# One shared branch for the slots beyond 64: gate/up and down products of a column group leave it together

## The chip, the cores and the metric

One core of one Trainium2 chip runs the whole program in one launch. The time is device microseconds of that core; the kernel before was timed three times (1551.54, 1560.07 and 1565.84 us, median 1560.07).

## The reference, cut to what matters

The program is two transformer blocks over 256 tokens of width 1024, all in float32. The first block has a mixer, a dense feed-forward layer, a second mixer and a layer of 8 experts; each token goes to 2 of the 8:

```
for e in range(8):
    out = out + gate[:, e] * (silu(h @ wg[e]) * (h @ wu[e])) @ wd[e]      # 1024 -> 2816 -> 1024
```

The second block has attention, a short convolution and a layer of 16 small experts in 4 groups; each token goes to one group and to 2 of its 4 experts:

```
hid = silu(h @ w_gate[e]) * (h @ w_up[e]) * combine[:, e]                 # 1024 -> 256
out = out + hid @ w_down[e]                                               # 256 -> 1024
```

How many tokens an expert (or a group) gets is known only when the router has run on the chip.

## The kernel before, in words

**Slots.** The tokens of an expert (first layer), or of a group (second layer), are gathered into up to 96 slots: the first 64, and 32 more. An integer flag per expert says whether more than 64 slots are in use; only the tensor engine reads it (`more_than_half`, L887). In this text an expert with more than 64 tokens is a *full* expert, the others are *half* experts. In the trace the products of the slots beyond 64 (the matmuls of shape 128\*32) run for experts 2, 4, 5 and 6 of the first layer and for the third of the four groups of the second layer.

**Order of the work.** The 2816 hidden columns of an expert are cut into six column groups, in the order 0, 5, 1, 2, 3, 4 (positions 0 to 5); group 5 has 256 columns, the others 512. A *gu unit* (`bin_unit`, L962) multiplies the gathered tokens with the gate and up columns of a group; a *dn unit* (`bin_down`, L1010) multiplies the hidden values of a group with its rows of the down matrix and adds to two PSUM banks per expert. `ffn_order` (L69) puts the dn unit of a column group behind the gu unit of the next: gu 0, dn of the expert before, gu 5, dn 0, gu 1, dn 5, and so on. In the second layer an expert is one gu unit of 256 columns (two loads) and one dn unit (one load), in the same interleaving.

**A gu unit** runs its main matmuls (slots 0 to 63; two column halves side by side, so 128\*64) into bank `a`, then a branch: where the flag is set, four 128\*32 matmuls per row for the slots beyond 64 into bank `b` (L978); else one matmul with zeros into `b` (L984). Then `bin_mul` (L988) makes silu(gate) x up in three parts, each an activation on ScalarE (L996) and a multiplication on VectorE (L997): part 0 from bank `a`, parts 1 and 2 from bank `b`. Parts 1 and 2 run for every expert, full or half.

**A dn unit** runs its main matmuls, then a branch of its own (L1018): the products of the slots beyond 64, and else nothing, or a matmul with zeros where it is the first dn unit of the expert. Behind the dn unit `turn_hid` calls `bin_hid` (L1000): the tensor engine transposes the hidden values just made, first those of part 0 (L1004), then those of parts 1 and 2 (L1006), ScalarE copies them (L1007), and the dn unit after the next gu unit reads them. The order of each engine's instructions is the program's; an instruction that waits holds up all behind it on its engine.

**The stream.** Weights come in 1 MB loads through SyncE's queue, in the order of use, into 11 buffers that serve both expert layers. A buffer is loaded again when the matmuls that read it are done (`Stream.retire`, L225, says so in the program's order). Rows of most other layers are split into a high and a low part, by ScalarE (L197) and VectorE (L198), some rows ahead of their use: `W.ahead` rows, `AHEAD` = 4, and `AH1` = 2 from the last column group of expert 7 on. Rows of the experts are used as loaded.

**The end of a layer** is `last_down` (L1077): the last dn unit, `bin_y` (L1028: the sums are copied out of PSUM, L1031 to L1033), then for each half of the tokens `scatter` (L1036: products with one-hot matrices, and the addition to `x`, L1053 or L1051) and the transposes of `x` for the next layer.

Of the kernel before, what the change touches and what calls it, by code (L numbers as in the profile page):

```python
# [18 lines left out]
P = 128  # L19
T = 256  # L20
D = 1024
KT = D // P
# [5 lines left out]
RAW = 5  # L28
ROWS = 6
AHEAD = 4  # L30
AH1 = 2
RATE = 8
PE_TAPS = 11
OVER1 = 2
HALF = 64
MORE = 32
# [27 lines left out]
LAST = GROUPS[-1]  # L64
# [180 lines left out]
def block_kernel(ctx: ExitStack, tc: tile.TileContext, stream, x_in, cst_in, cols_in, small_in, sgu_in,  # L245
# [42 lines left out]
    W = Stream(nc, wp, stream, stream_order(), gcol)  # L288
# [52 lines left out]
    def mm(o, a, b, start, stop):  # L341
        nc.tensor.matmul(o, a, b, start=start, stop=stop)  # L342
# [544 lines left out]
    def more_than_half(got, e):  # L887

        if ("reg", e) not in got:
            got["reg", e] = nc.values_load(  # L890
                got["more"][0:1, e:e + 1], engines=[mybir.EngineType.PE], min_val=0, max_val=1,
                skip_runtime_bounds_check_because="the flag is the result of a comparison")
        return got["reg", e]
# [58 lines left out]
    def to_slots(pm, i, src, n):  # L952
# [6 lines left out]
        nc.vector.tensor_copy(t.rearrange("p j n -> p (j n)"), b[:, 0:3 * n])  # L959
        return t  # L960

    def bin_unit(xT, more, n, hooks=()):  # L962


        a, b = ps("gu"), ps("gu")
        kc, m = 512 // n, n // 2
        todo = []
        for r in range(KT // kc):
            row = W.take()
            for j in range(kc):  # L970
                k, at = kc * r + j, 2 * n * j
                todo.append((k, row, at))
                for h in range(2):
                    mm(a[h * HALF:(h + 1) * HALF, 0:n], xT[:, k, 0:HALF], row[:, at + h * n:at + (h + 1) * n], k == 0,
                       k == KT - 1)
            if r < len(hooks) and hooks[r]:
                hooks[r]()
        with tc.If(more == 1) as c:  # L978
            for k, row, at in todo:
                for q in range(4):  # L980
                    c0 = at + (q % 2) * n + (q // 2) * m
                    mm(b[q * MORE:(q + 1) * MORE, 0:m], xT[:, k, HALF:CAP], row[:, c0:c0 + m], k == 0, k == KT - 1)
        with c.Else():
            mm(b[:, 0:m], zeros[:, 0:P], zeros[:, 0:m], True, True)  # L984
        W.retire(KT // kc)
        return a, b

    def bin_mul(banks, n, s, h, gate, up):  # L988


        m = n // 2
        for (b, c0, m, lo, w, to, g, u) in ((banks[0], 0, n, 0, HALF, HALF, gate[0], up[0]),
                                            (banks[1], n, m, 0, MORE, MORE, gate[1], up[1]),
                                            (banks[1], n + m, m, HALF, MORE, MORE, gate[1], up[1])):
            t, v = s[lo + w:lo + 2 * w, c0:c0 + m], h[to:to + w, c0:c0 + m]
            nc.scalar.activation(t, b[lo:lo + w, 0:m], AF.Silu, scale=g[lo:lo + w])  # L996
            nc.vector.scalar_tensor_tensor(v, b[lo + w:lo + 2 * w, 0:m], u[lo + w:lo + 2 * w], t, op0=ALU.mult,  # L997
                                           op1=ALU.mult)
# [11 lines left out]
    def bin_down(hT, nk, more, dn, first, last):  # L1010


        rws = [W.take() for _ in range(nk)]
        for k in range(nk):
            for h in range(2):
                mm(dn[0][h * HALF:(h + 1) * HALF], hT[:, k, 0:HALF], rws[k][:, h * 512:(h + 1) * 512], first and k == 0,
                   last and k == nk - 1)
        with tc.If(more == 1) as c:  # L1018
            for k in range(nk):
                for q in range(4):  # L1020
                    mm(dn[1][q * MORE:(q + 1) * MORE, 0:T], hT[:, k, HALF:CAP], rws[k][:, q * T:(q + 1) * T],
                       first and k == 0, last and k == nk - 1)
        if first:
            with c.Else():
                mm(dn[1][:, 0:T], zeros[:, 0:P], zeros, True, True)
        W.retire(nk)

    def bin_y(dn):  # L1028

# [46 lines left out]

    def last_down(hT, nk, more, dn, pt, i, gate, nxt, fill=None):  # L1077

        bin_down(hT, nk, more, dn, False, True)
        y = bin_y(dn)  # L1080

        def spread(tb):
            scatter(pt, i, y, tb, more, gate(tb) if gate else None, "ms" if fill else "gu")

        if fill:
            fill(0)
        spread(0)
        W.pump(2)
        if fill:
            fill(1)  # L1090
        nxt.half(0, 0)
        spread(1)
        if fill:
            fill(2)
        nxt.half(0, 1)
        W.ahead = AHEAD
        W.pump()

    def moe1(cur, nxt):
# [44 lines left out]
        def moe1_tiles():  # L1144
            return sl("k5", [D]), sl("k6", [D])

        hid, fresh, dn, ydone = {}, [], None, None
        for kind, e, g, _ in ffn_order(BASE_MOE, NE):
            if e == NE - 1 and g == LAST:
                W.ahead = AH1  # L1150
            p, i = divmod(e, 2)
            pos = GROUPS.index(g)
            n = 512 if g < 5 else 256
            if kind == "gu" and e == 0 and g in DENSE:
                kw = cur.lead(_03=lambda: (route(0), cur.parts(0)), _10=lambda: route(1), _11=lambda: cur.parts(1),
                              _13=place)
                kw["hooks"] = [None] * 4 + [lambda: gather_pair(0, [0]), lambda: gather_pair(0, [1, 2]),
                                            lambda: gather_pair(0, [3])]
                banks = (pair_unit if g < 5 else half_unit)(cur.T, **kw)
                fresh.append((e, g, n, act_mul(banks, n, ("t2", "t3"), [rs(cur.gi, tb) for tb in range(2)])))  # L1160
            elif kind == "gu":
                hooks = [None] * 8
                if i == 1 and p < 3 and pos == 1:
                    pmq[p + 1] = one_hots(got["posm"], p + 1)
                if fresh:
                    hooks[0:3] = [lambda: slots_T(0), turn_hid, weights]
                if i == 1 and p < 3 and pos >= 2:
                    hooks[3] = lambda p=p, q=pos - 2: gather_pair(p + 1, [q])
                if i == 1 and p < 3 and g == LAST:
                    hooks[6] = lambda p=p: slots_T(p + 1)  # L1170
                if ydone is not None and pos == 2:
                    for tb in range(2):
                        hooks[1 + 4 * tb] = lambda tb=tb, a=ydone: scatter_e(*a, tb)
                    ydone = None
                banks = bin_unit(XT[p][:, :, i], more_than_half(got, e), n, hooks=hooks)
                s, h = moe1_tiles()
                r = RS[e]
                bin_mul(banks, n, s, h, (r[:, 0], r[:, 1]), (r[:, 0], r[:, 2]))
                fresh.append((e, g, n, h))
            elif e == NE - 1 and g == LAST:  # L1180
                last_down(hid[e, g], 4, more_than_half(got, e), dn, PT[p], i, lambda tb: gates[:, tb, e:e + 1], nxt)
            else:
                nk = 4 if g < 5 else 2
                if pos == 0:
                    dn = [ps("dn"), ps("dn")]
                bin_down(hid[e, g], nk, more_than_half(got, e), dn, pos == 0, g == LAST)
                if g == LAST:
                    ydone = (e, bin_y(dn))
            if fresh and kind == "dn":
                turn_hid()  # L1190
            if kind == "dn" and e == OVER1 and g == LAST:
                over = past(got["posm"], gates, NE, "p1")
                overflow(got["flag"], cur, over, NE, N_FFN, BASE_MOE,
                         [(5, 4, 4, 0, 22), (1, 2, 2, 20, 32)],
                         "xa" if e % 4 == 0 else "xb")
                nxt.load()
# [226 lines left out]
    def moe2(cur, nxt, fill):  # L1423
# [99 lines left out]
            else:  # L1523
                hid[e] = bin_hid(hs, T, t)

        hid, fresh, dn, ydone = {}, [], None, None

        def scatter_g(g, y, tb):
            scatter(PT[g // 2], g % 2, y, tb, more_than_half(got, g))
# [1 line left out]
        for kind, e in expert_order(16):  # L1531
# [13 lines left out]
            elif kind == "gu":  # L1545
# [11 lines left out]
                if ydone is not None and e % 4 == 2:  # L1557
                    for tb in range(2):
                        hooks[2 * tb] = lambda tb=tb, a=ydone: scatter_g(*a, tb)
                    ydone = None  # L1560
                banks = bin_unit(XT[p][:, :, i], more_than_half(got, g), T, hooks=hooks)
                s, h = sl(f"t{e % 2}", [512]), sl(f"t{2 + e % 2}", [512])
                c, j = CS[g], e % 4
                bin_mul(banks, T, s, h, (c[:, 0, 4:5], c[:, 1, 4:5]), (c[:, 0, j:j + 1], c[:, 2, j:j + 1]))
                fresh.append((e, h))
            elif e == 15:
                last_down(hid[e], 2, more_than_half(got, g), dn, PT[p], i, None, nxt, fill)
            else:
                if e % 4 == 0:
                    dn = [ps("dn"), ps("dn")]  # L1570
                bin_down(hid[e], 2, more_than_half(got, g), dn, e % 4 == 0, e % 4 == 3)
                if e % 4 == 3:
                    ydone = (g, bin_y(dn))
            if fresh and kind == "dn":
# [183 lines left out]
```

## Time and profile before

| what | us |
|---|---|
| runs | 1551.54, 1565.84, 1560.07 |
| median | 1560.07 |
| the profiled execution | 1551.7 |
| its span, first to last instruction | 1549.9 |
| tensor engine busy | 1488.1 (96%) |
| VectorE busy | 629.0 (41%) |
| ScalarE busy | 523.5 (34%) |
| mean DMA share of the span (hardware queue 1) | 71.0% |

The span is cut in two by the expert layers: the first layer's sorted experts run from about 436 us to 1140 us, the second's from about 1376 us to 1510 us. An engine that is busy is not necessarily at its peak: matmuls overlap and their ends are modelled, so lost time shows as a larger distance between the starts of matmuls. Times on the left of a timeline row are counted from the span's start.

### The profile page before, as it was taken

What the parts mean: (1) busy time and instruction counts of PE and PEld (TensorE: products, weight loads), DVE (VectorE), ACT (ScalarE), POOL (GpSimd) and SP (SyncE); (2) the same over time, 40 slices, a digit from 0 to 9 for tenths busy, and PEclk for the clock granted to TensorE, in tenths of its full rate; (3) what the DMA queues carried; (4) which work ended last, traced back from release to release, by engine and by line L of the source; (5) the groups of instructions that cost most, each with busy time, mean ns of one, the idle gap of its engine ahead of it and who ended that gap; (6) DMA issues with size and microseconds to landing.
All of it is one profiled execution on the core that took longest, in us unless ns stands there. A gap on an engine that the chain in (4) does not pass through costs nothing. (4 is left out here: it accounts for less than half of the span.)

```text
span 1549.9 us, 22973 instructions
## 1 busy us (share of the span) xinstructions
PE 1488.1 (96%) x9434; PEld 903.9 (58%) x9434; DVE 629.0 (41%) x1136; ACT 523.5 (34%) x856; POOL 127.1 (8%) x106
## 2 busy tenths in 40 slices
PE   7899999999999999989999999999989999999998
PEld 5778888877843334434444444444347888865546
DVE  6986655698511211112111111111247566732235
ACT  7645544584421111111111111111136555622134
POOL 4804000052100000000000000000002000100000
PEclk9999999999999999999999999999999999999999
DMA  8424555533479999998999987899984345478870
GB/s 320 163 109 170 192 196 203 183 137 136 179 302 414 414 412 415 396 387 348 412 390 363 391 309 290 327 360 379 416 334 143 133 163 193 140 303 324 324 276 28
DMA packets 84088, 429.05 MB, mean 277 GB/s; under 512 B 9328, under 2 KB 9840, under 8 KB 53488
## 3 DMA queue, kind: packets, MB, share of 16 engines
q1 hardware_dynamic: 83232, 425.01, 71.0%
q8 instruction: 102, 1.67, 0.4%
q10 hardware_dynamic: 720, 2.10, 0.3%
q14 instruction: 34, 0.28, 0.0%
HBM read 426.02 MB, written 1.05 MB: 276 GB/s over the span
## 5 line engine op out<-in xcount | busy, mean ns | idle before, releaser
L997 DVE SCALAR_TENSOR_TENSOR k<-gu,slots,k 64x512 f32<-64x512 f32 (+1 forms) x141 | 76.7, 544 | 404.1 <-ACT k L996 403.4
L996 ACT ACTIVATE k<-gu,slots 64x512 f32<-64x512 f32 (+1 forms) x141 | 72.4, 513 | 356.0 <-PE gu L342 324.7
L342 PE MATMUL gu<-whi,xah 128*128 128x512 f32 x528 | 180.3, 404 | 6.1 <-ACT whi L197 4.0
L198 DVE SCALAR_TENSOR_TENSOR wlo<-raw,cols,whi 128x1024 fp32r<-128x1024 f32 (+1 forms) x146 | 160.8, 1140 | 49.6 <-ACT whi L197 49.5
L342 PE MATMUL gu<-wlo,xah 128*128 128x512 f32 x528 | 174.2, 394 | 1.4 <-POOL wlo L203 1.1
L342 PE MATMUL gu<-whi,xal 128*128 128x512 f32 x528 | 173.7, 393 | 0.9 <-DVE xal L457 0.9
L197 ACT ACTIVATE whi<-raw,cols 128x1024 fp32r<-128x1024 f32 (+1 forms) x146 | 142.6, 1027 | 27.7 <-PE gu L342 18.3
L342 PE MATMUL dn<-raw,k 128*64 128x512 f32 (+1 forms) x856 | 127.8, 498 | 1.9 <-DMA raw<-in_stream_dram 1.2
L446 POOL TENSOR_TENSOR rcol<-rnv,mhalf 128x1 f32<-128x1 f32 x16 | 8.9, 555 | 1309.4 <-DVE rnv L445 1309.4
L342 PEld LDWEIGHTS gu<-whi,xah 128*128 128x128 f32 x528 | 97.5, 190 | 28.4 <-ACT whi L197 4.7
L342 PEld LDWEIGHTS gu<-wlo,xah 128*128 128x128 f32 x528 | 99.9, 189 | 23.6 <-POOL wlo L203 1.6
L342 PEld LDWEIGHTS gu<-whi,xal 128*128 128x128 f32 x528 | 99.8, 189 | 22.9 <-DVE xal L457 1.5
L342 PE MATMUL gu<-raw,xah 128*64 128x256 f32 (+3 forms) x944 | 103.3, 409 | 5.5 <-PEq L859 5.1
L342 PE MATMUL gu<-raw,xbh 128*64 128x256 f32 (+3 forms) x800 | 100.9, 439 | 2.7 <-DMA raw<-in_stream_dram 2.2
L202 ACT ACTIVATE whi<-raw 128x1024 fp32r<-128x1024 f32 x70 | 72.5, 1056 | 36.3 <-PE gu L342 31.8
L342 PEld LDWEIGHTS dn<-raw,k 128*64 128x64 f32 (+1 forms) x856 | 41.6, 124 | 72.9 <-issue 59.9
L342 PE MATMUL gu<-whiraw,xah 128*32 128x256 f32 (+3 forms) x552 | 82.8, 453 | 0.5 <-PEq L1042 0.4
L342 PE MATMUL gu<-wloraw,xah 128*32 128x256 f32 (+3 forms) x552 | 81.4, 447 | 0.0
L1007 ACT ACTIVATE k<-ms 128x384 f32<-128x384 f32 (+1 forms) x61 | 26.4, 433 | 146.4 <-PE ms L1006 145.9
L342 PEld LDWEIGHTS gu<-raw,xah 128*64 128x64 f32 (+1 forms) x944 | 46.2, 124 | 50.3 <-issue 32.3
L342 PE MATMUL gu<-whiraw,xbh 128*32 128x256 f32 (+2 forms) x448 | 73.5, 482 | 1.7 <-PEq L859 0.9
L342 PE MATMUL gu<-wloraw,xbh 128*32 128x256 f32 (+2 forms) x448 | 73.3, 480 | 1.2 <-DMA wloraw<-in_stream_dram 1.1
(318 smaller groups left out, 1988.8 us busy)
## 6 DMA issues: line engine op xcount, KB each, us to landing
raw<-in_stream_dram SPq DMA_DIRECT2D x238, 1024.0 KB, 8.6
whiraw<-in_stream_dram SPq DMA_DIRECT2D x164, 512.0 KB, 9.9
wloraw<-in_stream_dram SPq DMA_DIRECT2D x164, 512.0 KB, 10.1
x<-in_x_dram SPq DMA_DIRECT2D x2, 512.0 KB, 6.0
k<-in_lnrow_dram ACTq DMA_DIRECT2D x2, 512.0 KB, 7.5
cst<-in_cst_dram SPq DMA_DIRECT2D x1, 593.0 KB, 14.9
k<-in_gains_dram ACTq DMA_DIRECT2D x1, 512.0 KB, 7.7
out_dram<-k SPq DMA_DIRECT2D x2, 256.0 KB, 2.0
```

Of the source, the lines that this page charges most:

```text
L197: nc.scalar.activation(hi[:, c], raw[:, c], AF.Copy, scale=g)
L198: nc.vector.scalar_tensor_tensor(lo[:, c], raw[:, c], g, hi[:, c], op0=ALU.mult, op1=ALU.subtract)
L202: nc.scalar.activation(hi, raw, AF.Copy)
L342: nc.tensor.matmul(o, a, b, start=start, stop=stop)
L446: nc.gpsimd.tensor_tensor(rs(gi, tb), v, mhalf[:, :1], op=ALU.pow)
L996: nc.scalar.activation(t, b[lo:lo + w, 0:m], AF.Silu, scale=g[lo:lo + w])
L997: nc.vector.scalar_tensor_tensor(v, b[lo + w:lo + 2 * w, 0:m], u[lo + w:lo + 2 * w], t, op0=ALU.mult, op1=ALU.mult)
L1007: nc.scalar.activation(hT[:, 0:n // P], b[:, 0:n // P], AF.Copy)
```

## The change: what it does

Where a gu unit is followed by a dn unit of the same expert (positions 1 to 5 of the first layer; every expert but the first of its group in the second), the gu unit's branch is taken out of it and put behind the main matmuls of that dn unit, into one branch with the dn unit's products beyond 64. Its else arm holds the gu unit's matmul with zeros, and the dn unit's where there is one. Part 0 of `bin_mul` stays behind the gu unit's main matmuls; parts 1 and 2 come behind the shared branch, ahead of `turn_hid`. The buffers of the gu unit's rows are given back behind the shared branch. `AH1` becomes 0, so that no row of the next layer is split ahead of `bin_y` of expert 7, and the `W.pump(2)` of `last_down` becomes a `W.pump(1)` behind the first transposes.

```diff
-AH1 = 2
+AH1 = 0
+    def the_others(*parts):
+        with tc.If(parts[0][0] == 1) as c:
+            for _, others, _, _ in parts:
+                others()
+        if any(p[2] for p in parts):
+            with c.Else():
+                for _, _, none, _ in parts:
+                    if none:
+                        none()
+        W.retire(sum(p[3] for p in parts))
     def bin_unit(xT, more, n, hooks=()):
...
-        with tc.If(more == 1) as c:
+        def others():
             for k, row, at in todo:
                 for q in range(4):
...
-        with c.Else():
+        def none():
             mm(b[:, 0:m], zeros[:, 0:P], zeros[:, 0:m], True, True)
-        W.retire(KT // kc)
-        return a, b
+        return (a, b), (more, others, none, KT // kc)
-    def bin_mul(banks, n, s, h, gate, up):
+    def bin_mul(part, banks, n, s, h, gate, up):
...
     def bin_down(hT, nk, more, dn, first, last):
...
-        W.retire(nk)
+        return more, others, none if first else None, nk
     def last_down(hT, nk, more, dn, pt, i, gate, nxt, fill=None):
-        bin_down(hT, nk, more, dn, False, True)
+        the_others(bin_down(hT, nk, more, dn, False, True))
         y = bin_y(dn)
...
         spread(0)
-        W.pump(2)
...
         nxt.half(0, 0)
+        W.pump(1)
         spread(1)
# gu units of the first layer (the second's likewise, with e % 4 == 0)
-                bin_mul(banks, n, s, h, (r[:, 0], r[:, 1]), (r[:, 0], r[:, 2]))
+                mul(slice(0, 1))
+                if pos == 0:
+                    the_others(later)
+                    mul(slice(1, 3))
+                else:
+                    held = later, mul
# dn units
-                bin_down(hid[e, g], nk, more_than_half(got, e), dn, pos == 0, g == LAST)
+                parts = [bin_down(hid[e, g], nk, more_than_half(got, e), dn, pos == 0, g == LAST)]
+                if held:
+                    parts.insert(0, held[0])
+                the_others(*parts)
+                if held:
+                    held[1](slice(1, 3))
+                held = None
```

## Rows read from the trace of the kernel before

**Rows 1.** Windows: engines' busy us (instructions), granted clock, DMA share, GB/s, four stretches.
```profile
489.50:578.50 89.00, 82.14 (x409) 31.26 (x407) 16.52 (x33) 16.26 (x33) 0.00 (x0) 0.98 1.02 413
672.70:762.90 90.20, 83.80 (x457) 36.18 (x455) 16.70 (x34) 16.37 (x33) 0.00 (x0) 0.96 0.95 374
762.90:1062.40 299.50, 298.73 (x2746) 129.62 (x2744) 43.17 (x79) 42.28 (x85) 0.00 (x0) 0.99 0.91 352
1383.80:1438.20 54.40, 51.37 (x331) 30.57 (x328) 13.99 (x35) 14.77 (x35) 0.00 (x0) 0.94 0.81 299
```

**Rows 2.** Timeline of TensorE (start, us, what, idle before): a dn unit, full expert.
```profile
834.10 1.08 PE L342 MATMUL dn<-whiraw,k 128*64 128x512 f32 x4
...
836.73 1.03 PE L342 MATMUL dn<-wloraw,k 128*64 128x512 f32 x4
837.69 0.64 PE L342 MATMUL dn<-whiraw,k 128*32 128x256 f32 x8
...
839.55 0.46 PE L1004 MATMUL ms<-ident,k 64*128 64x64 f32 x4
...
840.30 1.08 PE L342 MATMUL gu<-whiraw,xbh 128*64 128x512 f32 x4
```

**Rows 3.** The same view: gu and dn unit of a half expert, 512 columns.
```profile
1102.34 3.60 PE L342 MATMUL gu<-raw,xah 128*64 128x512 f32 x16
1105.87 0.39 PE L342 MATMUL gu<-zeros 128*128 128x256 f32 x1
1106.18 3.65 PE L342 MATMUL dn<-raw,k 128*64 128x512 f32 x16
1110.00 0.43 PE L1004 MATMUL ms<-ident,k 64*128 64x64 f32 x4 [0.16 <-PEq L1018]
...
1110.72 1.51 PE L342 MATMUL gu<-raw,xah 128*64 128x512 f32 x6
```

**Rows 4.** Timeline of all engines: end of a gu unit's 128\*32 matmuls, parts 1 and 2.
```profile
849.72 1.26 PE L342 MATMUL gu<-raw,xbh 128*32 128x256 f32 x20
...
851.04 0.47 ACT L996 ACTIVATE k<-gu,slots 32x256 f32<-32x256 f32 x1 [2.93 <-PE gu L342]
...
852.05 0.47 ACT L996 ACTIVATE k<-gu,slots 32x256 f32<-32x256 f32 x1 [0.55 <-DVE k L997]
...
852.55 0.49 DVE L997 SCALAR_TENSOR_TENSOR k<-gu,slots,k 32x256 f32<-32x256 f32 x1 [0.53 <-ACT k L996]
```

**Rows 5.** Groups by form: parts 1 and 2 in units of 256 columns (busy, mean ns).
```profile
L996 ACT ACTIVATE t<-gu,slots 32x128 f32<-32x128 f32 x28 | 10.0, 358 | 12.9 <-DVE t L997 7.1 <-PE gu L342 5.5
...
L997 DVE SCALAR_TENSOR_TENSOR t<-gu,slots,t 32x128 f32<-32x128 f32 x28 | 9.8, 350 | 11.3 <-ACT t L996 11.0
```

**Rows 6.** Timeline of TensorE: units of the second layer, half group.
```profile
1499.67 0.30 PE L1004 MATMUL ms<-ident,t 64*128 64x64 f32 x2 [0.16 <-DVE t L997]
...
1500.14 1.08 PE L342 MATMUL gu<-whiraw,xah 128*64 128x256 f32 x8
...
1503.74 0.33 PE L342 MATMUL gu<-zeros 128*128 128x128 f32 x1
1504.00 1.08 PE L342 MATMUL dn<-whiraw,k 128*64 128x512 f32 x4
...
1506.10 0.31 PE L1004 MATMUL ms<-ident,t 64*128 64x64 f32 x2 [0.16 <-DVE t L997]
```

**Rows 7.** Timeline of TensorE: expert 3's second gu unit, behind the overflow branch.
```profile
691.42 5.09 PE L342 MATMUL gu<-raw,xah 128*64 128x256 f32 x32 [5.09 <-PEq L859]
```

**Rows 8.** Timelines of ScalarE and TensorE: the end of the first expert layer.
```profile
1140.22 2.19 ACT L197 ACTIVATE whi<-raw,cols 128x1024 fp32r<-128x1024 f32 x2 [4.16 <-DMA raw<-in_stream_dram]
1142.31 0.57 ACT L1031 ACTIVATE k<-dn 64x512 f32<-64x512 f32 x1
...
1142.94 1.12 PE L342 MATMUL gu<-k,sguT 64*128 64x512 f32 x2 [3.18 <-ACT k L1031]
```

**Rows 9.** Instructions of L1018: duration ns min/median/max, first and last start us.
```profile
L1018 PEldq COMPARE_BRANCH  x92: 63/179/2589, 438.5 to 1508.1; - x92
```

More of the change, by code (lines that the diff above doesn't have):

```diff
@@ L993, in bin_mul @@
                                             (banks[1], n, m, 0, MORE, MORE, gate[1], up[1]),
-                                            (banks[1], n + m, m, HALF, MORE, MORE, gate[1], up[1])):
+                                            (banks[1], n + m, m, HALF, MORE, MORE, gate[1], up[1]))[part]:
             t, v = s[lo + w:lo + 2 * w, c0:c0 + m], h[to:to + w, c0:c0 + m]
@@ L1017, in bin_down, with others @@
                    last and k == nk - 1)
-        with tc.If(more == 1) as c:
+        def others():
             for k in range(nk):
@@ L1022, in bin_down, with none @@
                        first and k == 0, last and k == nk - 1)
-        if first:
-            with c.Else():
-                mm(dn[1][:, 0:T], zeros[:, 0:P], zeros, True, True)
-        W.retire(nk)
+        def none():
+            mm(dn[1][:, 0:T], zeros[:, 0:P], zeros, True, True)
+        return more, others, none if first else None, nk
     def bin_y(dn):
@@ L1145, in moe1_tiles @@
             return sl("k5", [D]), sl("k6", [D])
-        hid, fresh, dn, ydone = {}, [], None, None
+        hid, fresh, dn, ydone, held = {}, [], None, None, None
         for kind, e, g, _ in ffn_order(BASE_MOE, NE):
@@ L1174, in moe1, with mul @@
                     ydone = None
-                banks = bin_unit(XT[p][:, :, i], more_than_half(got, e), n, hooks=hooks)
+                banks, later = bin_unit(XT[p][:, :, i], more_than_half(got, e), n, hooks=hooks)
                 s, h = moe1_tiles()
                 r = RS[e]
-                bin_mul(banks, n, s, h, (r[:, 0], r[:, 1]), (r[:, 0], r[:, 2]))
+                def mul(part, a=(banks, n, s, h, (r[:, 0], r[:, 1]), (r[:, 0], r[:, 2]))):
+                    bin_mul(part, *a)
+                mul(slice(0, 1))
[4 more added lines that the diff above has]
+                    held = later, mul
                 fresh.append((e, g, n, h))
@@ L1524, in turn_hid @@
                 hid[e] = bin_hid(hs, T, t)
-        hid, fresh, dn, ydone = {}, [], None, None
+        hid, fresh, dn, ydone, held = {}, [], None, None, None
         def scatter_g(g, y, tb):
@@ L1560, in moe2, with mul @@
                     ydone = None
-                banks = bin_unit(XT[p][:, :, i], more_than_half(got, g), T, hooks=hooks)
+                banks, later = bin_unit(XT[p][:, :, i], more_than_half(got, g), T, hooks=hooks)
                 s, h = sl(f"t{e % 2}", [512]), sl(f"t{2 + e % 2}", [512])
                 c, j = CS[g], e % 4
-                bin_mul(banks, T, s, h, (c[:, 0, 4:5], c[:, 1, 4:5]), (c[:, 0, j:j + 1], c[:, 2, j:j + 1]))
+                def mul(part, a=(banks, T, s, h, (c[:, 0, 4:5], c[:, 1, 4:5]), (c[:, 0, j:j + 1], c[:, 2, j:j + 1]))):
+                    bin_mul(part, *a)
+                mul(slice(0, 1))
+                if e % 4 == 0:
+                    the_others(later)
+                    mul(slice(1, 3))
+                else:
+                    held = later, mul
                 fresh.append((e, h))
@@ L1570, in moe2 @@
                     dn = [ps("dn"), ps("dn")]
-                bin_down(hid[e], 2, more_than_half(got, g), dn, e % 4 == 0, e % 4 == 3)
+                parts = [bin_down(hid[e], 2, more_than_half(got, g), dn, e % 4 == 0, e % 4 == 3)]
+                if held:
+                    parts.insert(0, held[0])
+                the_others(*parts)
+                if held:
+                    held[1](slice(1, 3))
+                held = None
                 if e % 4 == 3:
```

## The prediction

> **What bounds the kernel now.** I read the stretches of the two expert layers first. In full experts the tensor engine is busy 298.7 of 299.5 us while the loads use 0.91 of the DMA engines; in the second layer it is busy 51.4 of 54.4 us at 0.81. Only expert 1 is held by its loads: 82.1 of 89.0 us busy at a DMA share of 1.02 [rows 1]. So what lengthens the tensor engine's own order of work lengthens the run, except in expert 1. VectorE and ScalarE are busy a fifth of the time or less there; they matter only where the tensor engine waits for them.
>
> How much expert 1 waits is seen against expert 3, which has the same work and hooks: 90.2 us [rows 1], of which 5.1 is the idle time behind the overflow branch and 1.4 the slow unit after it (5.09 us, where 8 rows of half the width of [rows 3] take 3.65) [rows 7], and 1.6 the products beyond 64 that the dn unit of expert 2 runs in that stretch (last main pair to transposes 2.39 us against 0.75) [rows 2, 3]. Without these expert 3 needs 82.1 us; expert 1 waits 89.0 - 82.1 = 6.9 us.
>
> **What a branch costs.** The jump itself is not seen in a full expert. A pair of main matmuls takes 0.43 us; from the last pair at 837.16 (836.73 + 0.43) to the first 128\*32 at 837.69 there are 0.53, so 0.1 us goes at this change of tile shape, and six pairs from 834.10 take 2.63 where 2.58 were due: 0.05 more for the first pair [rows 2]. In a half expert the dn unit's empty branch costs more: from the last pair (1106.18 + 3.06 = 1109.24) to the transposes 0.76 us, and 0.52 + 0.31 us stand around the matmul with zeros, where two main pairs would be 0.43 apart [rows 3].
>
> **Part 1, full experts** (5 units in each of 4 experts, 3 units in the second layer). Main follows main and others follow others: two changes of shape and one first pair go, -0.25 us a unit. Parts 1 and 2 now come with the dn unit's 128\*32 matmuls as their only cover. The chain is serial: the gu unit's matmuls end at 850.98, part 1 starts on ScalarE at 851.04, part 2's activation waits for VectorE's part 1, and the last multiplication ends at 853.04, so 2.06 us [rows 4]. With 0.06 until the transposes start and 0.2 for the last two of them, the next unit can start 2.32 us after the end of the gu unit's matmuls, 2.70 after the start of their last group (0.38 long). Without waiting it starts 0.22 (first group of the dn unit) + 1.51 (its other seven) + 0.31 + 0.75 (transposes) = 2.79 after that start [rows 2]. So nothing waits where the dn unit has four rows. Behind the group of 256 columns (position 2) the dn unit has two rows, 0.86 less cover: 2.70 - 1.93 = 0.77 lost, net +0.52. Sum 16 x -0.25 + 4 x 0.52 = -1.9 us. In the second layer, with two rows and the shorter copies of [rows 5], the same steps give +0.24 each, +0.7.
>
> **Part 2, half experts** (experts 0, 1, 3, 7: 20 units). Saved: gu to dn. From the last gu pair (1105.35) to the last dn pair (1109.24) now 3.89, then eight pairs, 3.44; from there to the transposes 0.76 now, 0.52 + 0.31 then: -0.37 us [rows 3]. Lost: parts 1 and 2 read the bank that the matmul with zeros fills, and that matmul now runs behind the dn unit. Before, the dn unit's 3.4 us covered the chain. Now from the start Z of the zeros: 0.39 for them [rows 3], 2.06 for the chain [rows 4], 0.06 and 0.2 as above: the next unit starts at Z + 2.71. Without waiting it would at Z + 0.31 + 0.72 = Z + 1.03 [rows 3]. The tensor engine waits 1.68 us in front of L1006, and all of the next gu unit is queued behind that wait. Net +1.3 us in 16 units of 512 columns, 20.8. At position 1 the copies are shorter and the dn unit's own matmul with zeros gives 0.1 more cover: +0.9 in 4 units, 3.6. Of these 24.4 us, the waits of expert 1 take up 7 (an estimate: the delays of experts 0 and 1, 12.2 together, fall into waits of 6.9): +17.4. The bounds are 12.2 (all of experts 0 and 1 hidden) and 24.4 (the loads late by as much).
>
> The Trainium skill, PSUM — Partial Sum Buffer, Terms, reports that different quadrants of one bank may be accessed by two engines at once; by that, part 2's activation needn't wait for VectorE, and the chain would be 0.5 us shorter. The trace decides against it: the activation starts when VectorE's part 1 has ended [rows 4], in the same instructions that the change keeps. By the page the whole sum would be about +6 us.
>
> **Part 3, second layer, half groups** (experts 2, 3, 5, 6, 7, 13, 14, 15). The chain is 0.06 + 2 x 0.358 + 2 x 0.350 + 3 x 0.03 = 1.57 us [rows 5]; after zeros of 0.33 the next unit starts at Z + 0.33 + 1.57 + 0.06 + 0.15 = Z + 2.11, without waiting at Z + 0.26 + 0.47 = Z + 0.73 [rows 6]: 1.38 lost, 0.39 saved by the steps of part 2, net +1.0. Three units (5, 6, 7) have a gather of the zeros' own shape ahead of them and save only about 0.15: +1.25. Sum +8.6. The loads are far from bounding here [rows 1], so nothing takes this up; the bounds are 5 (chain 0.5 shorter) and 11 (no saving).
>
> **Part 4, loads.** SyncE's queue issues in order, and each load waits for the matmuls that read its buffer. Those of a gu unit come free one dn unit later, 3.4 us. At 413 GB/s [rows 1] a load of 1 MB takes 2.5 us, 11 buffers 28 us; a column group holds 6 of them, so the other 5 (12.7 us) cover the delay. I take 0; if they don't, up to 3.4 us at the entries of experts 3 and 7.
>
> **Part 5, the end of the first layer.** ScalarE's split of two rows, 2.19 us, is ahead of the copy of the sums, and the tensor engine is idle 3.18 us [rows 8]. Without it the copy (0.57) and 0.1 of signalling remain: -2.5 us. What is late next: the first row is split behind the transposed first half, and rows 1 to 3 after it, 1.1 us each on ScalarE [rows 8] and as much on VectorE, against some 1.6 us of matmuls a row; I charge 0.5. Net -2, bounds -3.2 and 0 (the splits give all back).
>
> **Sum**: -1.9 + 17.4 + 8.6 + 0.7 - 2 = +22.8 us on the profiled execution's 1551.7, 1574.5. That execution is 8.4 us below the median of the runs; on the median it is 1582.9, so **1583 us**. By the bounds of parts 2 to 5 together it is some 1573 to 1593.
>
> **The rivals.**
> *Copies in time.* If the tensor engine reaches L1006 only when VectorE is through, the change gives its savings alone: 10 x -0.37 in experts 3 and 7, 20 x -0.25 in full ones, 11 x about -0.3 in the second layer, -2 at the end: -14 us, 1546. It decides at the wait of L1006: the tensor engine would have to need 1.7 us more from the zeros to these transposes than [rows 3] show. For it: today the trace shows next to no wait there. Against it: today's cover is exactly what is moved away. Chance 0.10, 0.06 of it under the 1% line.
> *Coarse wait.* If the copies wait for the end of the whole branch, in full experts too, the dn unit's 128\*32 matmuls (1.73 us) no longer cover: +1.65 in 16 units, +0.87 in 4 + 3: 32 more, 1615. It decides at part 1's start in full experts. Against it: now loads start on single rows inside the branch. Chance 0.08.
> *Loads bound the half experts.* If experts 3 and 7 hid their delays as expert 1 does, 12.4 less: +10, 1570. Against it: their stretches show no waits to take the delay up. Chance 0.05; with the PSUM page's rule (1566), 0.02 more.
> *Jumps.* A jump over the shared block stalls for its code. Now the longest of L1018's branches took 2.59 us [rows 9], hidden under 3.8 us of dn unit [rows 3] or 2.1 us in the second layer [rows 6]; 0.5 exposed in 8 units is +4, 1587, and were each stall twice as long 1.4 in 20 and 3.1 in 8, 1636. The Trainium skill, Runtime: NRT & Kernel Launch, Instruction fetch mechanics, says that a taken branch out of the window of fetched pages has to fetch its page first; a longer block makes that likelier. Chance 0.05.
>
> **How the numbers follow.** The forecast has 0.70. One per cent, 15.6 us, is what a measurement tells from no change; of the 0.70 I put 0.13 below it. Slower: 0.57 + 0.08 + 0.05 = 0.70. Within 1%: 0.13 + 0.04 + 0.05 + 0.02 = 0.24. Faster: 0.06. The range leaves out the first two rivals (0.18) and takes in the bounds: 1566 to 1595.
>
> **What would show it.** Right: in experts 3 and 7 each column group from position 2 on grows by about 1.3 us, with new waits of L1006 for L997 at its first and its last two transposes; full experts keep their period within 0.3 us; the wait of 3.18 us at the scatter shrinks below 1. Wrong: L1006 without such waits, or part 1 of full experts starting only after the dn unit's products.

## The result: 5% slower, more than three times the forecast

| what | before | after |
|---|---|---|
| median, us | 1557.96 (4 runs, 1551.54 to 1565.84) | 1637.76 (4 runs, 1633.24 to 1639.46) |
| ratio | | 1.0508, 95% interval 1.048 to 1.0536 |
| profiled execution (span) | 1551.7 (1549.9) | 1637.9 (1636.3) |
| mean granted clock of TensorE | 0.986 | 0.966 |

The forecast was 1583 us. Its half experts came out as worked out; its full experts didn't (some 30 us), and TensorE's granted clock, which it had not priced, took more than 20 us besides. Line numbers below are those of the changed kernel: the shared branch is L964, parts 0 to 2 of `bin_mul` are L1010 (ScalarE) and L1011 (VectorE), the transposes L1018 (part 0) and L1020 (parts 1 and 2), the copy of the sums L1047.

**Where the tensor engine waits now.** Groups by form of the changed kernel (line, engine, operation, count, busy us, mean ns, idle us ahead of them and its releaser):

```profile
L1020 PE MATMUL ms<-ident,k 32*128 32x32 f32 x172 | 26.6, 234 | 53.2 <-DVE k L1011 53.2
L1020 PE MATMUL ms<-ident,t 32*128 32x32 f32 x28 | 6.3, 241 | 13.5 <-DVE t L1011 13.5
```

The transposes of parts 1 and 2 have 66.7 us of idle time ahead of them, all of it ended by VectorE's multiplications. Before, the transposes at this place (L1006 there) had 0.8 us.

**A half expert**, timeline of all engines, the stretch that answers to [rows 3]:

```profile
494.15 1.46 PE L342 MATMUL dn<-raw,k 128*64 128x512 f32 x6
495.53 0.39 PE L342 MATMUL gu<-zeros 128*128 128x256 f32 x1
495.85 0.46 PE L1018 MATMUL ms<-ident,k 64*128 64x64 f32 x4
495.96 0.47 ACT L1010 ACTIVATE k<-gu,slots 32x256 f32<-32x256 f32 x1 [3.06 <-PE gu L342]
...
496.99 0.31 PE L1020 MATMUL ms<-ident,k 32*128 32x32 f32 x2 [0.68 <-DVE k L1011]
...
498.01 0.31 PE L1020 MATMUL ms<-ident,k 32*128 32x32 f32 x2 [0.71 <-DVE k L1011]
...
498.38 1.08 PE L342 MATMUL gu<-whiraw,xbh 128*64 128x512 f32 x4
```

This is the step that was forecast: the matmul with zeros stands behind the dn unit, the copies begin 0.43 us after its start, and the next gu unit starts 498.38 - 495.53 = 2.85 us after it; 2.71 was worked out.

**A full expert**, the same view; it answers to [rows 2, 4]:

```profile
649.04 0.83 PE L342 MATMUL gu<-raw,xah 128*32 128x256 f32 x12
649.69 1.91 PE L342 MATMUL dn<-raw,k 128*32 128x256 f32 x32
651.53 0.46 PE L1018 MATMUL ms<-ident,k 64*128 64x64 f32 x4
651.67 0.46 ACT L1010 ACTIVATE k<-gu,slots 32x256 f32<-32x256 f32 x1 [8.09 <-PE dn L342]
652.16 0.48 DVE L1011 SCALAR_TENSOR_TENSOR k<-gu,slots,k 32x256 f32<-32x256 f32 x1 [7.79 <-ACT k L1010]
652.67 0.46 ACT L1010 ACTIVATE k<-gu,slots 32x256 f32<-32x256 f32 x1 [0.55 <-DVE k L1011]
652.70 0.30 PE L1020 MATMUL ms<-ident,k 32*128 32x32 f32 x2 [0.71 <-DVE k L1011]
653.17 0.49 DVE L1011 SCALAR_TENSOR_TENSOR k<-gu,slots,k 32x256 f32<-32x256 f32 x1 [0.53 <-ACT k L1010]
653.72 0.30 PE L1020 MATMUL ms<-ident,k 32*128 32x32 f32 x2 [0.72 <-DVE k L1011]
```

The gu unit's products end at 649.87 (649.04 + 0.83). Yet part 1 starts at 651.67, just behind the last dn product (649.69 + 1.91 = 651.60), and its releaser is `dn`, a bank that it does not read. The 1.9 us of dn products that were to cover the copies cover nothing. That this holds throughout shows in the group of parts 1 and 2 (groups by form; the changed kernel): most of the idle time ahead of these copies is put down to `dn`.

```profile
L1010 ACT ACTIVATE k<-gu,slots 32x256 f32<-32x256 f32 x78 | 36.2, 464 | 199.2 <-PE dn L342 120.6 <-PE gu L342 56.4 <-DVE k L1011 22.1
```

**The clock.** Windows of the changed kernel (us, busy us of PE, PEld, DVE, ACT and POOL, granted clock, DMA share, GB/s). A window of a *group* runs from the first transposes of one unit's hidden values to those of the next; a *full group* is one of a full expert, a *half group* one of a half expert. The first two are full groups with the same waits; the next two the main matmuls of the gu unit in each of them, behind these waits, with a fall of the clock and without; then a half group, and a full and a half unit of the second layer:

```profile
651.53:671.42 19.89, 18.47 (x157) 7.50 (x153) 1.72 (x3) 2.10 (x4) 0.00 (x0) 0.91 0.79 315
858.52:876.71 18.19, 16.77 (x156) 7.09 (x153) 1.73 (x3) 2.10 (x4) 0.00 (x0) 1.00 0.90 347
653.95:662.14 8.19, 8.19 (x33) 2.61 (x33) 0.00 (x0) 0.49 (x1) 0.00 (x0) 0.79 1.01 414
860.94:867.44 6.50, 6.50 (x34) 2.22 (x34) 0.00 (x0) 0.49 (x1) 0.00 (x0) 1.00 1.02 418
1179.00:1192.15 13.15, 11.76 (x58) 4.26 (x57) 1.72 (x3) 2.10 (x4) 0.00 (x0) 1.00 1.00 373
1545.02:1554.97 9.95, 8.82 (x129) 5.41 (x125) 1.19 (x3) 1.51 (x4) 0.00 (x0) 1.00 0.96 339
1581.41:1588.84 7.43, 6.33 (x46) 3.43 (x46) 1.41 (x4) 2.82 (x6) 0.00 (x0) 1.00 0.40 143
```

A full group takes 18.19 us at full clock and 19.89 where the clock fell: 1.70 more, all of it in the gu unit behind the waits (8.19 us at 0.79 for 6.50 at 1.00): for part of that unit the engine runs at 1.2 instead of 2.4 GHz. Over the whole span the mean granted clock says how much was lost to the lower level: 0.034 of 1636.3 us is 56 us, and before 0.014 of 1549.9 is 22, so 34 us more (in the trace's clock records, 113 us at the lower level instead of 45).

**The end of the first layer**, ScalarE and TensorE, for [rows 8]:

```profile
1211.53 1.03 PE L342 MATMUL dn<-wloraw,k 128*64 128x512 f32 x4
1212.60 0.59 ACT L1047 ACTIVATE k<-dn 64x512 f32<-64x512 f32 x1 [3.75 <-PE dn L342]
...
1213.25 1.85 PE L342 MATMUL gu<-k,sguT 64*128 64x512 f32 x4 [0.69 <-ACT k L1047]
```

The split is out of the way of the copy, and the wait of 3.18 us is 0.69.

### The profile page after: what moved, and what is told of

Read it like the earlier page. It is cut to its first block, busy times and chain, and to the rows that moved or that the text cites. A ratio compares the mean times of both kernels' runs of the same rounds, so it can differ in the third digit from the quotient of the medians.

```text
span 1636.3 us, 22853 instructions
## 1 busy us (share of the span) xinstructions
PE 1518.0 (93%) x9434; PEld 927.2 (57%) x9434; DVE 629.0 (38%) x1136; ACT 523.5 (32%) x856; POOL 126.0 (8%) x106
## 3 DMA queue, kind: packets, MB, share of 16 engines
q8 instruction: 102, 1.67, 0.4%
## 5 line engine op out<-in xcount | busy, mean ns | idle before, releaser
L1011 DVE SCALAR_TENSOR_TENSOR k<-gu,slots,k 64x512 f32<-64x512 f32 (+1 forms) x141 | 76.7, 544 | 514.5 <-ACT k L1010 514.4
L1010 ACT ACTIVATE k<-gu,slots 64x512 f32<-64x512 f32 (+1 forms) x141 | 72.2, 512 | 519.8 <-PE gu L342 347.3
L342 PE MATMUL gu<-raw,xah 128*64 128x256 f32 (+3 forms) x944 | 107.6, 418 | 5.4 <-PEq L859 5.0
L342 PE MATMUL gu<-raw,xbh 128*64 128x256 f32 (+3 forms) x800 | 104.5, 447 | 0.4 <-PEq L1058 0.4
L342 PE MATMUL gu<-whiraw,xah 128*32 128x256 f32 (+3 forms) x552 | 90.6, 481 | 0.8 <-PEq L1058 0.4
L342 PE MATMUL gu<-wloraw,xah 128*32 128x256 f32 (+3 forms) x552 | 88.6, 472 | 0.0
L342 PEld LDWEIGHTS dn<-raw,k 128*64 128x64 f32 (+1 forms) x856 | 45.6, 126 | 71.1 <-issue 55.5
L342 PE MATMUL gu<-whiraw,xbh 128*32 128x256 f32 (+2 forms) x448 | 78.3, 500 | 2.1 <-PEq L859 1.2
L342 PE MATMUL gu<-wloraw,xbh 128*32 128x256 f32 (+2 forms) x448 | 78.8, 502 | 0.0
L1020 PE MATMUL ms<-ident,k 32*128 32x32 f32 x172 | 26.6, 234 | 53.2 <-DVE k L1011 53.2
```

Source lines behind the costliest of these rows:

```text
L1020: nc.tensor.transpose(b[:, f, HALF:CAP], h[MORE:HALF, n + f * P:n + (f + 1) * P], ident[MORE:HALF, MORE:HALF])
```

## The experiments

Two theories for the full experts. *Coarse wait*: a copy that reads a bank filled in a branch waits for the end of that branch, whatever else is in it. *Fine wait*, the prediction's: it waits for its own products, and the lost time has another cause. And for the rest: the waits lower the *clock*, or they don't.

**The end alone.** The kernel before with `AH1 = 0` and the moved pump:

```diff
-AH1 = 2
+AH1 = 0
         spread(0)
-        W.pump(2)
...
         nxt.half(0, 0)
+        W.pump(1)
         spread(1)
```

> The kernel before with the other half of the change alone: AH1 = 0 and the pump of one row behind the first transposed half; every gate/up and down product beyond 64 keeps its own branch, and the copies are those of before. By the prediction's part 5: 2 us faster than before (bounds 3.2 faster to 0), and the tensor engine's wait of 3.18 us at the scatter shrinks below 1. By the trace after the change, where the stretch from the last product of the first layer to the first product of the next projection takes 6.59 us instead of 12.35: 5.8 us faster. Rival: the rows that are split later delay the projection by as much, no change. By all three the slowing of some 80 us is not here.

Measured: 1553.82 us (12 runs) against 1557.81, ratio 0.997 (0.9954 to 0.9985). This half of the change gains 4 us (2 to 7), between the 2 and the 5.8 that were expected, and no kernel here is faster beyond the noise. Its windows give the undisturbed unit times of the order of before: a full and a half group of the first layer, a full and a half unit of the second.

```profile
639.97:656.78 16.81, 16.81 (x157) 6.83 (x153) 1.72 (x3) 2.10 (x4) 0.00 (x0) 1.00 0.97 382
1112.74:1124.62 11.88, 11.72 (x58) 4.11 (x58) 1.72 (x3) 2.10 (x4) 0.00 (x0) 1.00 1.02 412
1470.54:1479.40 8.86, 8.86 (x129) 5.19 (x125) 1.19 (x3) 1.51 (x4) 0.00 (x0) 1.00 0.99 332
1503.78:1510.21 6.43, 6.27 (x45) 3.27 (x46) 1.19 (x3) 1.90 (x5) 0.00 (x0) 1.00 0.38 143
```

**Two branches side by side.** The changed kernel, but with two branches where one was shared (both layers):

```diff
-                if held:
-                    parts.insert(0, held[0])
+                if held:
+                    the_others(held[0])
                 the_others(*parts)
```

> The changed kernel, but the gate/up products beyond 64 and the down products beyond 64 keep two branches, one right behind the other; the place of the gate/up products (behind the down unit's first 64) and the order of the copies stay as changed. Coarse wait (parts 1 and 2 of the copies start only when the branch that fills their bank has ended): in full experts that branch now ends 1.7 us earlier, the down products cover the copies, and their waits go: 32 us less by the prediction's price, about 6 more for the tile shape changes that come back, and the stretches at half clock in the full experts (16 more than before between 540 and 1250 us, 1.7 us each, 27 us) go with them: 1638 - 32 + 6 - 27 = 1585. Fine wait (the copies wait for their own products alone, and what holds the full experts is another thing): 1638 + 6. Half experts keep their waits by either.

Measured: 1589.43 us (1586.43 to 1600.51), ratio 1.023 (1.0197 to 1.0263); 1585 was expected by the coarse wait, 1644 by the fine. The order of products and copies is the changed kernel's; only a branch ends in between. Timeline of a full expert:

```profile
645.39 1.91 PE L342 MATMUL dn<-raw,k 128*32 128x256 f32 x32
645.64 0.47 ACT L1010 ACTIVATE k<-gu,slots 32x256 f32<-32x256 f32 x1 [6.36 <-PE gu L342]
...
647.15 0.49 DVE L1011 SCALAR_TENSOR_TENSOR k<-gu,slots,k 32x256 f32<-32x256 f32 x1 [0.53 <-ACT k L1010]
647.23 0.46 PE L1018 MATMUL ms<-ident,k 64*128 64x64 f32 x4
647.62 0.43 PE L1020 MATMUL ms<-ident,k 32*128 32x32 f32 x4
```

Part 1 now starts 0.25 us after the first dn product, released by `gu`, and the transposes don't wait. In the group of parts 1 and 2 no wait is put down to `dn` any more:

```profile
L1010 ACT ACTIVATE k<-gu,slots 32x256 f32<-32x256 f32 x78 | 36.3, 465 | 172.7 <-PE gu L342 150.4 <-DVE k L1011 22.1
```

That settles the coarse wait. The windows of two groups there, position 2 and the one behind it, and of a full unit of the second layer:

```profile
629.89:647.23 17.34, 16.71 (x157) 7.09 (x153) 2.06 (x5) 2.57 (x5) 0.00 (x0) 1.00 0.87 327
647.23:663.75 16.52, 16.52 (x156) 7.02 (x152) 1.72 (x4) 2.10 (x4) 0.00 (x0) 1.00 0.95 381
1494.00:1503.09 9.09, 8.75 (x128) 5.41 (x125) 1.19 (x4) 1.51 (x4) 0.00 (x0) 1.00 0.88 342
```

These are the prediction's own terms for full units: -0.29 (forecast -0.25), +0.53 at position 2 (+0.52), +0.23 in the second layer (+0.24). The "6 more" in the expectation was a slip: side by side, main still follows main and others follow others.

**Products of zeros in the waits.** The changed kernel with zeros multiplied ahead of the transposes that wait (`fill` is set for all but the first group of an expert):

```diff
+            if fill and f in (0, n // P // 2):
+                for _ in range(5 if n == 512 else 3):
+                    mm(bank[:, 4 * CAP:512], zeros[:, 0:P], zeros[:, 0:P], True, True)
             nc.tensor.transpose(b[:, f, HALF:CAP], ...
```

> The changed kernel with products of zeros ahead of the first and the third of the four transposes that wait for parts 1 and 2 (5 of 128 columns each time, 3 where the group is 256 wide, into 128 unused columns of the same bank), not at the first group of an expert. They lie in waits of some 0.7 us each and are meant to be shorter than these, so that the waits stay and the tensor engine is not idle in them. Clock theory (some 34 us of the 80 are stretches of 3.41 us at half clock that follow on the waits: 113 us at 0.5 against 45 before): the half-clock stretches fall back to about 45 us and the time to some 1605. Rival, waits alone (the clock's stretches have another cause or cost nothing): 1638 or a little more, half-clock stretches as in the changed kernel.

Measured: 1613.90 us (1609.21 to 1620.71), ratio 1.0362 (1.0332 to 1.0393), mean clock 0.978. First a row of the groups by form (L1024 is L1020 of the changed kernel), then the windows of a full and a half group:

```profile
L1024 PE MATMUL ms<-ident,k 32*128 32x32 f32 x172 | 26.5, 233 | 1.2
```

```profile
652.57:670.76 18.19, 18.18 (x166) 8.36 (x162) 1.72 (x3) 2.10 (x4) 0.00 (x0) 1.00 0.91 360
...
1158.88:1172.03 13.15, 13.14 (x68) 5.52 (x67) 1.72 (x3) 2.10 (x4) 0.00 (x0) 1.00 1.00 380
```

A group is as long as in the undisturbed groups of the changed kernel (18.19 and 13.15), so the copies still set its length; the engine is busy in the waits, 73 us instead of 113 run at half clock in the profiled execution, and 24 us are gone between the medians (1605 and 45 us at half clock had been expected). The clock theory holds: the waits cost more than their own length, by what the granted clock loses behind them.

**Two branches, and zeros in the half experts' waits.** Both edits above, the second for experts 0, 1, 3 and 7 and the half groups only. This is the kernel that the prediction had priced.

> Two branches side by side as in two_branches (1589.4), and products of zeros in the waits of the half experts' transposes alone (5 of 128 columns ahead of the first and of the third of the four, 3 where the group is 256 wide). This is the kernel that the prediction priced, without the clock that the waits cost: copies covered in full experts, 1.3 us lost in each half unit. If the prediction's terms are right and only the coarse wait and the clock are missing: 1583 (1573 to 1590), with the half units at 13.16 and 7.43 us as now. If the waits' clock costs nothing in half experts: 1589 as two_branches.

Measured: 1583.73 us (1579.61 to 1584.28), ratio 1.0163 (1.0138 to 1.0188); the forecast was 1583. That the two agree to 1 us is in part luck, since differences of 1.5 to 4 us in the terms cancel (the table below). Windows of a full and a half group, and of experts 0 and 1 together:

```profile
644.41:660.92 16.51, 16.51 (x156) 7.01 (x152) 1.72 (x4) 2.10 (x4) 0.00 (x0) 1.00 0.99 379
1109.50:1122.73 13.23, 13.08 (x68) 5.53 (x68) 1.72 (x3) 2.11 (x5) 0.00 (x0) 1.00 1.01 386
...
441.92:599.09 157.17, 155.00 (x837) 69.32 (x836) 25.83 (x50) 27.35 (x56) 0.00 (x0) 0.97 1.00 399
```

With two branches the zeros are 0.08 us too long in a half group (13.23 for 13.15), some 2 us in 28 units.

**Sharing in full experts alone.** Two branches side by side, and only there; everything else in the order of before, the end as changed. Of its edits this one sets the limit (the second layer likewise, with `g != 2`); the other is that of the two branches above:

```diff
-                if pos == 0:
+                if pos == 0 or e not in (2, 4, 5, 6):
                     the_others(later)
```

> The changed kernel with the sharing in full experts and full groups alone (experts 2, 4, 5, 6 and the third group of the second layer, fixed by number), there with two branches side by side; all other units are in the order of before, and the end of the first layer is as changed. In the profile of two_branches a full column group takes 16.52 us instead of 16.81. Savings theory (part 1 of the prediction: two changes of tile shape and a first pair go, 0.25 us a unit): 23 x 0.25 to 0.29 = 6 us and 4.0 at the end: 1558 - 10 = 1548, period 16.5, no waits of the transposes beyond 64. Rival, the sharing costs in itself (jumps over the moved blocks, loads that come a down unit later): 1554, which the end alone gives, or above.

Measured: 1554.13 us (12 runs) against 1558.29, ratio 0.9979 (0.9964 to 0.9993). Its windows (position 2, then position 3):

```profile
620.36:637.69 17.33, 16.70 (x156) 7.09 (x153) 2.05 (x5) 2.57 (x5) 0.00 (x0) 1.00 0.96 366
637.69:654.21 16.52, 16.52 (x156) 7.02 (x153) 1.72 (x4) 2.10 (x4) 0.00 (x0) 1.00 0.96 382
```

The expectation, 1548, forgot position 2 and the second layer. With the unit times of the profiles, an expert gains 4 x 0.29 - 0.52 = 0.64 and the three units of the second layer together lose 0.9: 1.7 us in all, not 6; part 1 of the prediction had 1.9 less 0.7. From 1553.8, which the end alone gives, 1552 was due; the intervals of the two kernels overlap. The savings per unit are there and the medians don't show them. The listed runs show where they can have gone: their mean granted clock is 0.9804, that of the end alone 0.9835 (the kernel before has 0.980 beside either), some 5 us more lost to the lower level.

**Late transposes.** The changed kernel with `turn_hid` behind the third row of the next gu unit (the second layer likewise):

```diff
-            if fresh and kind == "dn":
+            if fresh and kind == "dn" and (units[at + 1][0] == "dn" or (e == OVER1 and g == LAST)):
                 turn_hid()
...
+                if fresh and turn_hid not in hooks:
+                    hooks[2] = lambda was=hooks[2]: (turn_hid(), was and was())
                 banks, later = bin_unit(...)
```

> The changed kernel, but the transposes of a unit's hidden values run behind the third row of the next gate/up unit instead of ahead of it, so that 2.6 us of matmuls cover the copies of parts 1 and 2 in every unit with a successor (two units at the ends and two ahead of the overflow products stay as changed). If the waits of these transposes and what they do to the clock are all of the slowing: no waits, half-clock stretches as before, and the change's savings alone: 5.8 at the end of the first layer, 0.2 to 0.3 in some 50 units less 0.1 to 0.2 for one more change of tile shape: 1558 - 6 - 5 = 1547 (1540 to 1556). If the sharing of the branch costs in itself (jumps, loads that come later): above 1570.

Measured: 1563.48 us (1560.57 to 1568.49), ratio 1.004 (1.0023 to 1.0057). The waits are all but gone (5.3 us of 66.7 are left, in the units whose transposes stay where they were) and with them 74 of the 80 us, but 1547 was expected. To see whether the sharing or the late transposes cost the rest, the same late transposes with no sharing:

```diff
# on the kernel before
-AH1 = 2
+AH1 = 0
...
+                    hooks[2] = lambda was=hooks[2]: (turn_hid(), was and was())
                 banks = bin_unit(...)
```

> The kernel before with the end of the first layer as changed and the transposes of a unit's hidden values behind the third row of the next gate/up unit, with no sharing: each of the products beyond 64 in its own branch where it was before. late_turn is this and the sharing (1563.5 instead of the 1547 expected). If the late transposes cost by themselves 0.15 us a unit (one more change of tile shape; the full column group takes 16.67 us in late_turn and 16.52 in two_branches): 1554 + 50 x 0.15 = 1561, waits for loads in experts 0 and 1 as before (2.2 us in all). If instead the sharing is what costs in late_turn (loads released one down unit later; its waits for loads are 5.5 us): 1554 here, and the 5.5 us of waits for loads do not come.

Measured: 1564.09 us (1559.32 to 1567.92), ratio 1.0035 (1.0018 to 1.0051). Windows of a full and a half group, first of this kernel:

```profile
645.56:662.52 16.96, 16.96 (x154) 6.74 (x153) 1.72 (x3) 2.10 (x4) 0.00 (x0) 1.00 0.94 360
1113.43:1125.48 12.05, 11.89 (x60) 4.16 (x58) 1.72 (x3) 2.10 (x4) 0.00 (x0) 1.00 1.01 382
```

then of the late transposes with sharing, and behind them its waits for loads (us in total, times, longest):

```profile
649.03:665.70 16.67, 16.67 (x155) 6.93 (x153) 1.73 (x3) 2.10 (x4) 0.00 (x0) 1.00 0.93 365
1107.19:1118.86 11.67, 11.67 (x59) 4.10 (x57) 1.72 (x3) 2.10 (x4) 0.00 (x0) 1.00 1.02 410
```

```profile
PE gu L342 <- DMA raw<-in_stream_dram: 5.5, 7, 1.4
...
PE dn L342 <- DMA raw<-in_stream_dram: 3.7, 7, 0.7
```

Transposes in the middle of a gu unit cost 0.15 to 0.17 us a unit by themselves (16.96 for 16.81, 12.05 for 11.88); over the 50 and more such units that is some 8 of the 10.3 us by which this kernel is over the end alone. The 1547 had this cost in it, as 0.1 to 0.2 us a unit. What it counted and the medians don't show is the saving by the sharing: 0.29 and 0.38 us a unit in these rows, but 0.6 us between the medians. Waits for loads take some of it back (9.2 us with sharing; 5.2 without, by the same two rows of that kernel's waits: 4.1 and 1.1), and the granted clock can have taken as much: 0.978 in the mean of the six runs with sharing, 0.981 in the ten without, 5 us. Where the rest is was not found; it stays open. The profiles of the two differ by some us in stretches that the edit does not touch, too.

## Why the prediction was wrong, step by step

The medians form a chain, each kernel a step on from the one before it (each step is uncertain by some 3 to 6 us, from the intervals; that the steps sum to the whole is true of any chain, so it is the unit times above that bear the readings). The last column says how much the two kernels of a step lost to the lower clock: span x (1 - granted clock), in the mean of the listed runs (uncertain by about 1 us for the kernels with 12 and more runs and for the changed one, by 2 to 4 for the two with zeros).

| step | from, to (us) | measured | prediction | lost to the clock |
|---|---|---|---|---|
| end of the layer | 1557.8, 1553.8 | -4.0 | -2 | 31, 26 |
| full units, copies covered | 1553.8, 1554.1 | +0.3 | -1.9 + 0.7 | 26, 30 |
| half units, both layers (waits filled) | 1554.1, 1583.7 | +29.6 (2 of it the zeros) | +17.4 + 8.6 | 30, 32 |
| full units: coarse wait (waits filled) | 1583.7, 1613.9 | +30.2 | none; +32 as a rival of chance 0.08 | 32, 29 |
| clock: waits not filled | 1613.9, 1637.8 | +23.9 | none | 29, 56 |

So the steps of the half units and of the coarse wait are all but free of the clock and the last is the clock alone; in the first two steps, which are small, the clock moved as much as the time did, and how much of them it is was not separated.

**The step that failed** is in part 1: "Parts 1 and 2 now come with the dn unit's 128\*32 matmuls as their only cover ... So nothing waits where the dn unit has four rows." The cover is none: in the changed kernel the copies wait for the end of the branch that holds both. The rival *Coarse wait* had the mechanism, the place and the size: its 1.65 us a unit against 18.19 - 16.52 = 1.67 measured, its 1.11 in the second layer (0.87 on the 0.24 of part 1) against 9.95 - 8.86 = 1.09. What was held against it, that "now loads start on single rows inside the branch", was no argument: a load that is released from inside a branch is no sign that a copy is. In the changed kernel loads start inside the shared branch too, row by row, the first 0.06 us after a row's products (646.21 + 0.64 = 646.85), in the very unit whose part 1 waits until 651.67:

```profile
646.91 0.33 SPq L171 DMA_DIRECT2D whiraw<-in_stream_dram  x1
647.34 0.37 SPq L171 DMA_DIRECT2D wloraw<-in_stream_dram  x1
```

The trace of before could not decide it, because each branch held one unit's products and its end was also theirs ([rows 4] fits both theories). When a trace fits two readings and the change makes them differ, 0.08 is too little.

**The clock** was in no part and no rival. The prediction priced each wait at its own length. The windows of before showed a granted clock of 0.94 to 0.98 in the three stretches that have idle time in them, and 0.99 where the engine is busy throughout [rows 1]; that was the hint. A plainer one was expert 3's unit behind the overflow branch, which the prediction set aside as "the slow unit" (5.09 us for 3.65 [rows 7]). In the window of that unit (kernel before) the granted clock is 0.71:

```profile
691.40:696.50 5.10, 5.08 (x33) 3.19 (x33) 0.00 (x0) 0.00 (x0) 0.00 (x0) 0.71 1.03 384
```

The clock made 24 us of 80.

**Part 2** (half experts) was right: 11.88 to 13.15 us a group, +1.27, where +1.31 had been worked out, with the waits of 0.68 and 0.71 us at the two places named. The Trainium skill, PSUM — Partial Sum Buffer, Terms, reports that different quadrants of one bank may be accessed at the same time. No run here tests that of the chip; the trace says only that this program doesn't use it, which was all that the forecast needed: ScalarE idles 0.55 us between part 1 and part 2, until VectorE's multiplication of part 1 has ended, in half and full experts. Experts 0 and 1 showed 6.6 us of their 12.2, where 5.2 was estimated: together they took 150.57 us before (442.41 to 592.98, clock 0.99) and 157.17 with two branches and zeros (clock 0.97); two hundredths of the clock are 3 us of it.

**Part 3** was right: 6.43 to 7.43 us in a half unit of the second layer, +1.0 as worked out, and over the layer too: from the first to the last transposes of hidden values it is 118.9 us with sharing in full experts alone (1384.62 to 1503.53) and 127.4 with two branches and zeros (1403.44 to 1530.88), +8.5 where +8.6 was forecast. **Part 4**, which took the delay of the loads at nothing, held in the changed kernel, whose tensor engine waits more for copies; with the waits gone, in the late transposes, loads that come later do show (the 9.2 us above).

**Part 5**: the wait went from 3.18 to 0.69 us, 2.5 as worked out. From the start of the last dn product to that of the next projection's first it was 12.4 us before (1139.16 to 1151.52) and 8.1 in the end alone (1143.62 to 1151.75). The scatter's first four products took 1.26 us from first to last start instead of 2.54; before, there was a wait of 0.60 us among them, and the granted clock was 0.56 for the last two. Measured were -4.0 us (-7 to -2), against -2; the loss to the clock went down by 6 us with it (table above), and whether the 0.5 that was charged for later rows came can't be told.

**Jumps**: no more than before. The longest branch of L964 took 4.0 us, but the tensor engine's waits that the profile puts down to that line are 1.2 us in six. The Trainium skill, Runtime: NRT & Kernel Launch, Instruction fetch mechanics, says that a jump out of the fetched window pays for its page; no run here shows such a price in the tensor engine's time for the longer block.

## What to carry to other kernels

Merging two conditional blocks merged their ends in this kernel: the copies, which read a result of the first, then waited for the second. Before such an edit ask of each consumer which instruction releases it now, and look for a case in the trace where "its own product" and "the end of its block" lie apart; if there is none, give both readings a real chance, or keep two blocks side by side, which here cost nothing that can be measured. And a wait on a tensor engine that is otherwise full can cost more than its length: look at the granted clock of stretches that already have such waits.

## What the runs showed of the hardware that was not expected

- Two waits of some 0.7 us, 0.3 us of transposes between them, were followed by a fall to half clock (1.2 GHz) in most full groups of the changed kernel, in seven of the nine at positions 3 to 5 of experts 2, 4 and 6, and not in the others with the same waits (651.53 and 858.52 above). Products whose results nobody reads, put into the waits, brought 24 us back.
- Copies on ScalarE that read a bank filled in a conditional block started only at the block's end (651.67), while loads for buffers read in the same block started row by row inside it (646.91). Whether that lies with the chip or with how the program is built, no run here tells.
- The granted clock also differs between executions of the same instructions: the first transposes of hidden values of expert 0 start at 442.4 us in the kernel before and at 447.1 in the one with zeros in the waits, though both run the same work up to there (clock 0.99 and 0.98 in the first 440 us). So single profiles differ by some us for no reason of the kernel's, and a saving of 2 us shows in unit times but not in medians.
